# When VectorE reads the sums at the turn of the down projection's two passes, and which product a seven-product chunk begins with

## The chip, the cores and the metric

One core of a Trainium2 chip runs the whole program. The metric is the device time of one execution in microseconds (us), here the median of three runs. One further execution was taken by the hardware profiler; all rows below are from that one.

## What is computed

One decoder layer on 256 tokens of width 2048, in float32: a projection, two kinds of attention, an output projection, a layer norm, a gated FFN with a short convolution, and a second layer norm. The change lies in the FFN's second half alone:

```python
def conv_ffn(h, w_up, conv_w, conv_b, w_down):
    u = h @ w_up
    g, val = u[..., :FFN_DIM], u[..., FFN_DIM:]
    ...
    return (jax.nn.silu(gc) * val) @ w_down          # 256x5632 times 5632x2048

f = conv_ffn(h, w_up[l], conv_w[l], conv_b[l], w_down[l])
h = layer_norm(DEEPNORM_ALPHA * h + f, ln2_g[l], ln2_b[l])
```

## The kernel before

Each float32 factor is split into a rounded high part and the low rest (`hi`, `lo`), and a product is three matmuls: high by high, high by low, low by high. ScalarE (ACT) makes the high part, VectorE (DVE) subtracts to get the low one. All engines run instruction lists that the code writes out in order; an engine that waits for one instruction holds back all that stand behind it.

The down projection `act @ w_down` is done in two passes n = 0 and 1, one for each half of the 2048 output columns. A pass goes over 22 chunks p = 0 to 21 of 256 FFN features. "Chunk 0/21" below is chunk 21 of pass 0. A plain chunk (`mm_d`) is 24 matmuls, in 12 pairs that alternate between two PSUM banks: first the 12 of token row t = 0 (`bank[0]`, `bank[1]`; `CB[0]`), then the 12 of row t = 1 (`bank[2]`, `bank[3]`; `CB[1]`). The chunks that `SEVEN` lists (3, 6, 9, 12, 15, 18 in pass 0) are done by Strassen's scheme instead: `mm_seven` makes seven products of three matmuls, 21 in all. Its right-hand sides are seven blocks in the tile `slot`, 0 to 2 raw blocks of the weight chunk, 3 to 6 sums of blocks. The left-hand sides are blocks of activations or their sums (`sums`, with `sh` for the high and `sl` for the low parts). Products 1, 5, 6, 7 collect in banks 4, 5, 6, 7 (`MB`) and products 2, 3, 4 directly in the `CB` banks.

What a seven-product chunk s needs is made in the two chunks ahead of it. In `begin(s - 2)` ScalarE writes the negated high parts of raw blocks 0 to 2 into the low half of `slot` (L516), and a transfer issued by GpSimd's queue adds the raw blocks to them in place (L517): the low parts of blocks 0 to 2 come from this transfer. VectorE makes the sums (L519, L520, L492 to L495) there, and in `middle(s - 2)` their low parts (L529, L505), the next block sum (L536) and other splits. The last block follows in `begin(s - 1)`.

Weight chunks come into four `raw` buffers. SyncE's queue (SP) issues the load of chunk i + 6 in `begin(i)`; it waits there until the buffer of chunk i + 2 is free. For a seven-product chunk that is when L517's transfer and L536 have read it, and the loads behind it in SP's queue wait too. So loads go out in bursts of three, each begun when a transfer of L517 has landed. In chunk 1/9 the two vectors of the last layer norm (`load_gb`, L392, two transfers of 1024 KB) are issued as well.

At the turn of the passes the `CB` banks of pass 0 must be added into `z` (`z_add`, L871) before pass 1 writes them again. The code does it within chunk 0/21 and before chunk 1/0:

```python
            for k in range(2):
                mm_d(i, 0, [0, 1], k)
            if n == 0 and p == PT - 1:
                for c in range(2):
                    z_add(0, 0, c, CB[0][c])
            if i < last[0] - 1:
                middle(i)
            for k in range(2):
                mm_d(i, 1, [0, 1], k)
```

The two `z_add` of row 1 follow after that. `shared_out` adds the `MB` banks into `z` in the two chunks behind the last seven-product chunk of a pass, and `z_stats` takes statistics of `z` in the two chunks after the turn. The last four chunks of pass 1 run in another order (`mm_d` by column, `mm_d_end`) with high and low parts that are made in chunk 1/17 (tile `end`).

Of the kernel before, what the change touches and what calls it, by code (L numbers as in the profile page):

```python
# [41 lines left out]
PAIRED_END = 4  # L42
PT = FT // 2

SEVEN = (range(3, 19, 3), range(1, 14, 3))

ENDS = {(1, 1): ("cos_d", "sin_d"), (2, 0): ("mask", "cos_m"), (2, 1): ("sin_m", "lam4")}

# [2 lines left out]
def hymba_layer(ctx: ExitStack, tc: tile.TileContext, a: dict):  # L51
# [72 lines left out]
    def split(i, half, both=None):  # L124

        if i >= NS or (i, half) in parts:
            return
        t = loaded[i] if half == 0 else loaded.pop(i)
        if both is None:
            hi = splits.tile([P, 1024], F32R, name="hi")  # L130
            lo = splits.tile([P, 1024], F32R, name="lo")
        else:
            hi, lo = both[:, half], both[:, 2 + half]
        for x, y in pieces(i, half):
            if i < 4 and x % 512 == 0:
                split_x(4 * i + x // 512, 4 * i + (y + 511) // 512)
            s = slice(x - 1024 * half, y - 1024 * half)
            ACT.activation(hi[:, s], t[:, x:y], AF.Copy)  # L138
            DVE.tensor_tensor(lo[:, s], t[:, x:y], hi[:, s].bitcast(F32), ALU.subtract)  # L139
        parts[i, half] = (hi, lo)  # L140
# [101 lines left out]
    def at(step, fn, *args, rank=LATER):  # L242
        after.setdefault(step, []).append((rank, len(after.get(step, ())), fn, args))
# [144 lines left out]
    def load_gb(which, both):  # L388
        for j, n in enumerate(("g", "b")):
            t = both[:, j]  # L390
            src = a[f"ln{which}_{n}"]
            SP.dma_start(t, bass.AP(tensor=src.tensor, offset=src.offset, ap=[[0, P], [1, D]]))  # L392
            gb[n] = t
# [60 lines left out]
    def seven(i):  # L454
        return stream[i][0] == "d" and stream[i][1] in SEVEN[stream[i][2]]

# [16 lines left out]
    def split_act(i, k):  # L473

        if i >= NS or stream[i][0] != "d" or (i, k) in aparts:
            return
        src = act_of(2 * stream[i][1] + k)
        hi, lo = act_tiles(i, k)
        ACT.activation(hi, src, AF.Copy)
        DVE.tensor_tensor(lo, src, hi.bitcast(F32), ALU.subtract)  # L480
        aparts[i, k] = (hi, lo)
# [16 lines left out]
    def act_sums_split(i):  # L498
        f = sums[i]
        out = []  # L500
        for j in range(2):
            hi = keep.tile([P, 2, P], F32R, name="sh", tag=("mask", "cos_m")[j])
            lo = keep.tile([P, 2, P], F32R, name="sl", tag=("sin_m", "lam4")[j])
            ACT.activation(hi, f[j], AF.Copy)
            DVE.tensor_tensor(lo, f[j], hi.bitcast(F32), ALU.subtract)  # L505
            out += [(hi[:, k], lo[:, k]) for k in range(2)]

        sums[i] = out
# [17 lines left out]
    def blocks_lo(i, *js):  # L526
        slot, f = blocks[i]
        for j in js:
            DVE.tensor_tensor(slot[:, 1, 3 + j], f[j % 2 if j < 2 else 0], slot[:, 0, 3 + j].bitcast(F32),  # L529
                              ALU.subtract)  # L530

    def blocks_sum(i, j):

        t = loaded[i].rearrange("p (b c) -> p b c", c=512)
        f = blocks[i][1]
        DVE.tensor_tensor(f[0], t[:, 2 - j], f[0], ALU.subtract)  # L536
        if j == 1:
            loaded.pop(i)

    def blocks_hi(i, j):  # L540
        slot, f = blocks[i]
        ACT.activation(slot[:, 0, 5 + j], f[0], AF.Copy)
# [15 lines left out]
    def begin(i):  # L558

        urgent(i)  # L560
        j = i + 2
        split_act(j - 1, 1)
        split_act(j, 0)
        if j < NS and seven(j):
            blocks_raw(j)
            act_sums(j)
        elif j - 1 < NS and seven(j - 1):
            blocks_sum(j - 1, 1)
            split(j, 1)
            blocks_hi(j - 1, 1)  # L570
            blocks_lo(j - 1, 3)
        else:
            split(j, 1)
        load(i + 6)
        pending(i)

    def middle(i):

        urgent(i + 0.5)
        if i + 2 < NS and seven(i + 2):  # L580
            blocks_lo(i + 2, 0)
            blocks_sum(i + 2, 0)
            blocks_lo(i + 2, 1)
            act_sums_split(i + 2)
            blocks_hi(i + 2, 0)
            split(i + 3, 0)
            blocks_lo(i + 2, 2)
        elif i + 3 < NS and not seven(i + 3):
            split(i + 3, 0)
        pending(i + 0.5)  # L590

    def urgent(i):
        for _, _, fn, args in sorted((x for x in after.get(i, ()) if x[0] < LATER), key=lambda x: x[:2]):
            fn(*args)

    def pending(i):
        for x in after.pop(i, ()):
            if x[0] == LATER:
                x[2](*x[3])

    def done(i):
        for half in range(2):
            parts.pop((i, half))
# [68 lines left out]
    last = range(first_u - PAIRED, first_u)  # L672
# [169 lines left out]
    def mm_three(key, dst, lhs, rhs):  # L842
        for x, y in ((0, 0), (0, 1), (1, 0)):
            mm_count(key, dst, lhs[x], rhs[y])

    def mm_d(i, t, cs, k):

        n = stream[i][2]
        ts = slice(t * P, (t + 1) * P)
        ah, al = (x[:, ts] for x in aparts[i, k])  # L850
        w = [weights(i, (1536 * c if k == 0 else 512 + 512 * c), 512) for c in cs]
        for lhs, j in ((ah, 0), (ah, 1), (al, 0)):
            for c, wc in zip(cs, w):
                mm_count((n, t, c), CB[t][c], lhs, wc[j])

    def mm_seven(i):
        n = stream[i][2]
        slot, _ = blocks.pop(i)
        s3, s1, s2, s4 = sums.pop(i)
        (h0, l0), (h1, l1) = aparts[i, 0], aparts[i, 1]  # L860
        a11, a12, a22 = (h0[:, 0:P], l0[:, 0:P]), (h1[:, 0:P], l1[:, 0:P]), (h1[:, P:], l1[:, P:])
        for m, lhs, b in ((1, a11, 0), (2, a12, 1), (5, s1, 3), (7, s3, 4), (6, s2, 5), (3, s4, 2), (4, a22, 6)):
            t, c = {2: (0, 0), 3: (0, 1), 4: (1, 0)}.get(m, (None, None))
            key, dst = ((n, m), MB[m]) if t is None else ((n, t, c), CB[t][c])
            if m == 6:
                middle(i)
            mm_three(key, dst, lhs, (slot[:, 0, b], slot[:, 1, b]))

    def z_add(n, t, c, src, alpha=1.0):
        s = slice((2 * n + c) * 512, (2 * n + c + 1) * 512)  # L870
        DVE.scalar_tensor_tensor(z[:, t, s], z[:, t, s], alpha, src, op0=ALU.mult, op1=ALU.add)  # L871
# [23 lines left out]
    last = range(NS - PAIRED_END, NS)  # L895


    for n in range(2):
        np_ = PT if n == 0 else PT - PAIRED_END
        n7 = len(SEVEN[n])  # L900
        for m in MB:
# [18 lines left out]
    for i in range(first_d, NS - PAIRED_END):  # L920
        begin(i)
        _, p, n, _ = stream[i]
        if n == 1 and p == 9:
            load_gb(2, keep.tile([P, 2, D], F32, name="gb2", tag="ma"))
        if i == last[0] - 1:
            split_act(last[1], 1)
            for j, g in ((last[2], "t2"), (last[3], "mb")):
                end = keep.tile([P, 4, 1024], F32R, name="end", tag=g)
                for k in range(2):
                    split_act(j, k)  # L930
                    split(j, k, end)
        if seven(i):
            mm_seven(i)
            if p == SEVEN[n][-1]:
                at(i + 1, shared_out, n, 0)
                at(i + 2, shared_out, n, 1)
        else:
            for k in range(2):
                mm_d(i, 0, [0, 1], k)
            if n == 0 and p == PT - 1:  # L940
                for c in range(2):
                    z_add(0, 0, c, CB[0][c])
            if i < last[0] - 1:
                middle(i)
            for k in range(2):
                mm_d(i, 1, [0, 1], k)
            done(i)
            if n == 0 and p == PT - 1:
                for c in range(2):
                    z_add(0, 1, c, CB[1][c])  # L950
                for t in range(2):
                    for c in range(2):
                        at(i + 2 + t, z_stats, t, c, (512, 256)[t])
        for k in range(2):
            aparts.pop((i, k))
# [58 lines left out]
    for o in (1024, 1280):  # L1014
        s = slice(o, o + 256)
        b = bank[2][:, o - 1024:o - 768]
# [72 lines left out]
```

## Time and profile before

| what | value |
|---|---|
| median of 3 runs | 1144.22 us (1143.83 to 1145.06) |
| the profiled execution, its own time | 1144.3 us |
| its span, first to last instruction | 1142.5 us |
| TensorE (PE) busy | 1124.0 us, 98% |
| VectorE busy | 810.2 us, 71% |
| ScalarE busy | 614.6 us, 54% |
| granted TensorE clock, mean | 0.997 of full speed |

TensorE is busy in nearly all of the span, so what can be won without taking matmuls out is only the time in which it stands still; the places are few and can be looked at one by one.

### The profile page before, as it was taken

The page shows a single profiled execution, that of the slowest core. Times are in us where ns is not written, and L with a number is a line of the kernel's source. Part 1 is how long each engine was busy: PE and PEld are TensorE (multiplying, and loading weights), DVE is VectorE, ACT ScalarE, POOL GpSimd, SP SyncE. Part 2 cuts the span into 40 slices and gives each one's busy share as a digit, 9 for nine tenths or more (in the row PEclk, how much of TensorE's full clock was granted, in tenths as well). Part 3 has the DMA queues.
Part 4 walks back from the last instruction along what each step waited for, and adds up shares of the span by engine and source line. Part 5 has one row for each costly group of instructions (what it writes and reads, how often), then busy time and mean ns, then how long its engine had stood idle before and what let it go on. Part 6 is the DMA issues. An engine that isn't in the chain of part 4 may idle for free.

```text
span 1142.5 us, 15605 instructions
## 1 busy us (share of the span) xinstructions
PE 1124.0 (98%) x5971; PEld 961.2 (84%) x5971; DVE 810.2 (71%) x1373; ACT 614.6 (54%) x1007; POOL 30.2 (3%) x38
## 2 busy tenths in 40 slices
PE   9999999999999999999999999999999999999996
PEld 6888888888888898888888888888888888877785
DVE  6895886857745777777666566666656788898885
ACT  6565564444443485554545555454555667666751
POOL 0000000000000000000000000000000000000004
PEclk9999999999999999999999999999999999999998
DMA  9755454454455456555555555555555678877841
GB/s 319 292 221 193 151 182 167 165 184 175 157 184 184 185 200 231 194 186 185 184 190 193 202 189 184 185 186 191 192 202 178 208 210 254 277 197 227 279 173 74
DMA packets 47324, 226.56 MB, mean 198 GB/s; under 512 B 4625, under 2 KB 6545, under 8 KB 27665
## 3 DMA queue, kind: packets, MB, share of 16 engines
q1 hardware_dynamic: 45664, 216.92, 53.5%
q0 software_dynamic: 1584, 8.65, 3.8%
q8 instruction: 46, 0.75, 0.3%
q14 instruction: 30, 0.24, 0.1%
HBM read 214.80 MB, written 2.10 MB: 190 GB/s over the span
## 4 chain that ended last, share of the span: by engine, by line
PE 93%; DMA 3%; DVE 2%; ACT 1%; issue 0%; SPq 0%; POOL 0%; ACTq 0%
PE bank L206 92%; DMA slot<-raw 2%; DMA raw<-in_w_v 1%; PE bank L329 0%; DVE z L871 0%; DVE lo L139 0%; ACT slot L516 0%; ACT hi L138 0%; DVE z L976 0%; PE bank L705 0%; SPq L155 0%; PE bank L376 0%; SPq L121 0%; ACT hf L708 0%; DVE h L720 0%
## 5 line engine op out<-in xcount | busy, mean ns | idle before, releaser
L139 DVE TENSOR_TENSOR lo<-raw,hi 128x1024 fp32r<-128x1024 f32 (+1 forms) x372 | 440.8, 1200 | 216.5 <-ACT hi L138 216.2
L138 ACT ACTIVATE hi<-raw 128x1024 fp32r<-128x1024 f32 (+1 forms) x372 | 380.1, 1035 | 230.0 <-PE bank L206 198.3
L206 PE MATMUL bank<-h,hi 128*128 128x512 f32 x1376 | 477.2, 390 | 0.0
L206 PE MATMUL bank<-h,lo 128*128 128x256 f32 x1376 | 388.4, 282 | 0.0
L206 PEld LDWEIGHTS bank<-h,hi 128*128 128x128 f32 x1376 | 258.3, 188 | 53.4
L206 PEld LDWEIGHTS bank<-h,lo 128*128 128x128 f32 x1376 | 260.8, 190 | 0.0
L206 PE MATMUL bank<-x,hi 128*128 128x512 f32 x512 | 181.6, 396 | 0.0
L206 PE MATMUL bank<-x,lo 128*128 128x256 f32 x512 | 144.4, 282 | 0.0
L206 PEld LDWEIGHTS bank<-x,hi 128*128 128x128 f32 x512 | 96.2, 188 | 21.4 <-issue 1.3
L206 PEld LDWEIGHTS bank<-x,lo 128*128 128x128 f32 x512 | 97.0, 190 | 0.2
L206 PE MATMUL bank<-hi,x 128*128 128x512 f32 x256 | 85.3, 403 | 0.6 <-ACT hi L138 0.6
L206 PEld LDWEIGHTS bank<-hi,x 128*128 128x128 f32 x256 | 48.2, 188 | 13.3 <-ACT hi L138 2.1
L443 ACT ACTIVATE gc<-gs,vec 128x256 f32<-128x256 f32 x43 | 25.9, 602 | 58.6 <-DVE gs L220 58.6
L206 PE MATMUL bank<-lo,x 128*128 128x512 f32 x128 | 51.1, 399 | 0.8 <-DVE lo L139 0.8
L446 ACT ACTIVATE gc<-gc 128x256 f32<-128x256 f32 x44 | 18.4, 418 | 48.9 <-DVE gc L445 48.9
L206 PE MATMUL bank<-hi,ah 128*128 128x512 f32 (+1 forms) x126 | 40.6, 396 | 2.4 <-DVE z L871 2.3
L206 PE MATMUL bank<-hi,mh 128*128 128x512 f32 x128 | 42.2, 400 | 0.0
L206 PE MATMUL bank<-lo,mh 128*128 128x512 f32 x128 | 41.6, 396 | 0.0
L206 PE MATMUL bank<-hi,ml 128*128 128x512 f32 x128 | 41.6, 396 | 0.0
L444 DVE SCALAR_TENSOR_TENSOR gc<-gs,vec,gc 128x255 f32<-128x255 f32 x43 | 20.8, 484 | 28.8 <-ACT gc L443 28.8
L206 PE MATMUL bank<-lo,ah 128*128 128x512 f32 (+1 forms) x126 | 39.7, 390 | 0.0
L206 PE MATMUL bank<-hi,al 128*128 128x512 f32 (+1 forms) x126 | 39.7, 390 | 0.0
(176 smaller groups left out, 1284.9 us busy)
## 6 DMA issues: line engine op xcount, KB each, us to landing
raw<-in_w_u SPq DMA_DIRECT2D x88, 1024.0 KB, 4.8
raw<-in_w_d SPq DMA_DIRECT2D x88, 512.0 KB, 5.9
raw<-in_w_qk SPq DMA_DIRECT2D x32, 1024.0 KB, 4.8
raw<-in_w_o SPq DMA_DIRECT2D x16, 1024.0 KB, 4.8
raw<-in_w_v SPq DMA_DIRECT2D x12, 1024.0 KB, 4.8
slot<-raw POOLq DMA_DIRECT2D x11, 768.0 KB, 7.3
raw<-in_w_v SPq DMA_DIRECT2D x8, 256.0 KB, 5.6
raw<-in_w_v SPq DMA_DIRECT2D x4, 512.0 KB, 7.7
```

What stands on the lines that cost most here:

```text
L138: ACT.activation(hi[:, s], t[:, x:y], AF.Copy)
L139: DVE.tensor_tensor(lo[:, s], t[:, x:y], hi[:, s].bitcast(F32), ALU.subtract)
L206: PE.matmul(out, lhsT, rhs, start=start, stop=stop)
L443: ACT.activation(gc, g, AF.Identity, bias=vec[:, C_CB + f:C_CB + f + 1], scale=w[2])
L444: DVE.scalar_tensor_tensor(gc[:, 1:], g[:, 0:S - 1], w[1], gc[:, 1:], op0=ALU.mult, op1=ALU.add)
L446: ACT.activation(gc, gc, AF.Silu)
```

## The change

Three edits. In pass 1 the seven-product chunks move by one, from 1, 4, 7, 10, 13 to 2, 5, 8, 11, 14. In every seven-product chunk, of both passes, products 5 and 7 come first, ahead of 1 and 2. And in chunk 0/21 `middle` is called after the `z_add` of row 1 and not between the two rows.

```diff
-SEVEN = (range(3, 19, 3), range(1, 14, 3))
+SEVEN = (range(3, 19, 3), range(2, 15, 3))
...
-        for m, lhs, b in ((1, a11, 0), (2, a12, 1), (5, s1, 3), (7, s3, 4), (6, s2, 5), (3, s4, 2), (4, a22, 6)):
+        for m, lhs, b in ((5, s1, 3), (7, s3, 4), (1, a11, 0), (2, a12, 1), (6, s2, 5), (3, s4, 2), (4, a22, 6)):
...
             if n == 0 and p == PT - 1:
                 for c in range(2):
                     z_add(0, 0, c, CB[0][c])
-            if i < last[0] - 1:
+            elif i < last[0] - 1:
                 middle(i)
             for k in range(2):
                 mm_d(i, 1, [0, 1], k)
...
             if n == 0 and p == PT - 1:
                 for c in range(2):
                     z_add(0, 1, c, CB[1][c])
+                middle(i)
                 for t in range(2):
```

VectorE's list at the turn, before: `bank_72` to `bank_75` are the `CB` banks 0 to 3 (row 0, then row 1), `slot`, `tf`, `sl` belong to the seven-product chunk 1/1, `lo<-raw` is the low part of a plain chunk's weights.

```order
L871 SCALAR_TENSOR_TENSOR z<-z,bank_72 128x512
L871 SCALAR_TENSOR_TENSOR z<-z,bank_73 128x512
L529 TENSOR_TENSOR slot<-tf,slot 128x512
L536 TENSOR_TENSOR tf<-raw,tf 128x512
L529 TENSOR_TENSOR slot<-tf,slot 128x512
L505 TENSOR_TENSOR sl<-sf,sh 128x256 x2
L139 TENSOR_TENSOR lo<-raw,hi 128x1024
L529 TENSOR_TENSOR slot<-tf,slot 128x512
L871 SCALAR_TENSOR_TENSOR z<-z,bank_74 128x512
L871 SCALAR_TENSOR_TENSOR z<-z,bank_75 128x512
```

The same place of the changed kernel, from the end of `shared_out` (the first row adds its last part) on; the two `lo` are those of chunk 1/1, which is a plain chunk now:

```order
L871 SCALAR_TENSOR_TENSOR z<-z,act_6820 128x512 x2
L139 TENSOR_TENSOR lo<-raw,hi 128x1024
L480 TENSOR_TENSOR bl<-act_3772,bh 128x256
L480 TENSOR_TENSOR al<-act_3772,ah 128x256
L139 TENSOR_TENSOR lo<-raw,hi 128x1024
L871 SCALAR_TENSOR_TENSOR z<-z,bank_72 128x512
L871 SCALAR_TENSOR_TENSOR z<-z,bank_73 128x512
L871 SCALAR_TENSOR_TENSOR z<-z,bank_74 128x512
L871 SCALAR_TENSOR_TENSOR z<-z,bank_75 128x512
L480 TENSOR_TENSOR bl<-act_3772,bh 128x256
L480 TENSOR_TENSOR al<-act_3772,ah 128x256
L519 TENSOR_TENSOR tf<-raw 128x512
```

Nothing stands between the rows of `z` any more, the two low parts of weights stand ahead of them, and the sums that now belong to chunk 1/2 stand behind.

TensorE's list in a seven-product chunk, the difference (`bank_77` and `bank_79` are banks 5 and 7, products 5 and 7; `bank_76` is product 1, `bank_72` product 2):

```order
+L206 MATMUL bank_77<-slot,sh 128x512 x2
+L206 MATMUL bank_77<-slot,sl 128x512
+L206 MATMUL bank_79<-slot,sh 128x512 x2
+L206 MATMUL bank_79<-slot,sl 128x512
 L206 MATMUL bank_76<-slot,ah 128x512 x2
 L206 MATMUL bank_76<-slot,al 128x512
 L206 MATMUL bank_72<-slot,bh 128x512 x2
 L206 MATMUL bank_72<-slot,bl 128x512
-L206 MATMUL bank_77<-slot,sh 128x512 x2
-L206 MATMUL bank_77<-slot,sl 128x512
-L206 MATMUL bank_79<-slot,sh 128x512 x2
-L206 MATMUL bank_79<-slot,sl 128x512
```

Six matmuls on sums of blocks moved ahead of the first product that reads a low part of a raw block.

## Rows read from the trace of the kernel before

**Rows 1.** The page's first line.
```profile
span 1142.5 us, 15605 instructions
```

**Rows 2.** Waits of PE: who for whom, us in total, times, longest.
```profile
PE bank L206 <- DVE z L871: 2.3, 1, 2.3
PE bank L206 <- DMA slot<-raw: 1.7, 2, 1.3
```

**Rows 3.** Timeline of PE at the turn: start us, us, instruction, count.
```profile
1004.59 0.64 PE L206 MATMUL bank<-hi,ah 128*128 128x512 f32 x2
...
1007.36 0.64 PE L206 MATMUL bank<-hi,ah 128*128 128x512 f32 x2
...
1009.66 0.61 PE L206 MATMUL bank<-hi,bl 128*128 128x512 f32 x2
1012.62 1.09 PE L206 MATMUL bank<-hi,ah 128*128 128x512 f32 x2 [2.35 <-DVE z L871]
1013.55 0.62 PE L206 MATMUL bank<-lo,ah 128*128 128x512 f32 x2
```

**Rows 4.** Timeline of PE where chunks 1/7 and 1/13 begin.
```profile
1047.77 0.40 PE L206 MATMUL bank<-slot,ah 128*128 128x512 f32 x1
...
1048.94 0.39 PE L206 MATMUL bank<-slot,al 128*128 128x512 f32 x1
...
1080.39 0.40 PE L206 MATMUL bank<-slot,ah 128*128 128x512 f32 x1
...
1082.41 0.39 PE L206 MATMUL bank<-slot,al 128*128 128x512 f32 x1
```

**Rows 5.** Stretches: us, busy of PE, PEld, DVE, ACT, POOL, PEclk, DMA share, GB/s.
```profile
1007.36:1015.85 8.49, 6.04 (x26) 4.43 (x24) 8.08 (x14) 4.74 (x8) 0.00 (x0) 1.00 0.25 46
```

**Rows 6.** Timeline of DVE at the turn.
```profile
1001.75 1.29 DVE L871 SCALAR_TENSOR_TENSOR z<-z,act 128x512 f32<-128x512 f32 x2
1002.96 0.42 DVE L480 TENSOR_TENSOR bl<-act,bh 128x256 fp32r<-128x256 f32 x1
1003.29 0.42 DVE L480 TENSOR_TENSOR al<-act,ah 128x256 fp32r<-128x256 f32 x1
...
1010.14 1.23 DVE L139 TENSOR_TENSOR lo<-raw,hi 128x1024 fp32r<-128x1024 f32 x1 [0.37 <-ACT hi L138]
1011.28 0.68 DVE L529 TENSOR_TENSOR slot<-tf,slot 128x512 fp32r<-128x512 f32 x1
1011.89 1.28 DVE L871 SCALAR_TENSOR_TENSOR z<-z,bank 128x512 f32<-128x512 f32 x2
```

**Rows 7.** The chain that ended last: start us, us, what.
```profile
1039.12 9.44 DMA slot<-raw
...
1071.75 10.28 DMA slot<-raw
```

**Rows 8.** Timeline of ACT, the split that follows chunk 0/19.
```profile
996.26 1.06 ACT L138 ACTIVATE hi<-raw 128x1024 fp32r<-128x1024 f32 x1 [3.33 <-PE bank L206]
```

**Rows 9.** Line L517, from issue to landing of its 11 transfers.
```profile
DMA to landing us min/median/max: 5.7/7.3/10.3
```

**Rows 10.** SP's issues: a weight chunk is L114 and L115.
```profile
1036.33 0.38 SPq L114 DMA_DIRECT2D raw<-in_w_d  x1
...
1063.40 0.38 SPq L114 DMA_DIRECT2D raw<-in_w_d  x1
...
1065.34 0.74 SPq L392 DMA_DIRECT2D gb<-in_ln_g  x1
...
1067.85 0.38 SPq L114 DMA_DIRECT2D raw<-in_w_d  x1
```

**Rows 11.** Timeline of DVE: sums' low parts for 1/4; the first `end` part.
```profile
1027.39 0.76 DVE L505 TENSOR_TENSOR sl<-sf,sh 128x256 fp32r<-128x256 f32 x2
...
1108.12 1.22 DVE L139 TENSOR_TENSOR end<-raw,end 128x1024 fp32r<-128x1024 f32 x1
```

**Rows 12.** Timeline of PE, the first matmul that reads `end`.
```profile
1111.77 1.56 PE L206 MATMUL bank<-end,eh 128*128 128x512 f32 x6
```

## The prediction

> **What bounds the kernel now.** I read the page's busy shares first: the span is 1142.5 us [rows 1] and TensorE is busy in 98% of it. The change takes no matmul out, so it can win only where TensorE stands still. The view of waits therefore came next, for PE alone. Of its waits two lines lie in the part of the program that changes: 2.3 us, once, for a `z_add`, and 1.7 us in two pieces for the transfer into `slot` [rows 2]. The timeline of PE then gives the true price of each, because a wait also costs a slow restart. A pair of matmuls takes 0.46 us: from 1007.36 to 1009.66 there are five pairs in 2.30 us [rows 3].
>
> - The turn: from the last pair of row 0 in chunk 1/0 (1009.66) to the second pair of row 1 (1013.55) it is 3.89 us, where two pairs take 0.92 [rows 3]. Lost: 2.97 us.
> - Chunk 1/7: from the first matmul (1047.77) to the third (1048.94) it is 1.17 us instead of 0.46 [rows 4]. Lost: 0.71 us.
> - Chunk 1/13: 1080.39 to 1082.41, 2.02 us [rows 4]. Lost: 1.56 us.
>
> Together 5.24 us. The granted clock stayed at 1.00, the level of 2.4 GHz, in the stretch that holds the longest of these stops [rows 5], so no gain or loss by the clock is to be added.
>
> **The turn, part by part.** Row 1 of chunk 1/0 may start when VectorE has read banks 2 and 3. These were complete when chunk 0/21 ended, at about 1007.4, but the reads ran only from 1011.89 on, since the block sums, a weight split and their waits for ScalarE stood ahead of them; TensorE restarted at 1012.62, when the first of the two was through [rows 3, 6]. The change puts `middle` behind the reads and, by moving the seven-product chunk from 1/1 to 1/2, also takes the sums of `begin(0/21)` out of the way. What stands there now is a plain chunk's preparation: two `lo`, one ahead and one behind a `bl` and `al`. I work out when VectorE comes to each read.
>
> The first `hi` of chunk 1/1 needs the split buffer of chunk 0/20. One chunk earlier ScalarE began the like at 996.26, as soon as PE released it [rows 8]; a plain chunk is 12 pairs, 5.54 us, so it begins at 1001.80 and ends at 1002.86. VectorE finishes `shared_out` at 1003.04 [rows 6], so ScalarE is not late. From start to start a `lo` takes 1.14 us (1010.14 to 1011.28), `bl` and `al` 0.33 each (1002.96 to 1003.29), the two adds of a row 1.28 [rows 6]. Hence 1003.04 + 1.14 + 0.67 + 1.14 = 1005.99 for the first read of row 0, and 1007.27 for the end of the second. TensorE wants bank 0 at 1007.36 and bank 1 a matmul (0.23 us) later [rows 3]: 0.3 us to spare at bank 1, 0.7 at bank 0. This is tight, and it is a rival below. Row 1 is complete at about 1007.5, its reads end at 1008.8, and TensorE wants bank 2 at 1010.12 (1007.36 plus six pairs): 1.3 us to spare. I take the whole 2.97 us as gained; the bounds are nothing (the wait returns in full at row 0) and 2.97.
>
> What goes late instead: the sums for 1/2 begin behind these reads, at 1008.8, which is 1.4 us into chunk 1/0; even counted from that chunk's start they are no more than 1.4 us late. For 1/4 the low parts of the sums were ready at 1027.39 + 0.76 = 1028.15 [rows 11], and that chunk began 15.96 us (two plain chunks and 21 products) before 1/7, at 1031.81 [rows 4]. That leaves 3.7 us, which covers it. Cost taken: 0. If the cover were gone, each us would be a us of TensorE.
>
> **Products 5 and 7 first.** They read only sums, not the blocks whose low parts the transfer writes. Before, the second matmul needed the transfer: in 1/13 it was due at 1080.62, 8.87 us after the issue at 1071.75 [rows 4, 7]. Now six matmuls, three pairs or 1.38 us, come ahead, so the transfer may take 10.25 us. It took 9.44 ahead of 1/7 and 10.28 ahead of 1/13 [rows 7], and 7.3 in the median of 11 [rows 9]. With the same transfers the 0.71 us vanishes and of the 1.56 us some 0.03 stays.
>
> They need not be the same transfers, since the chunks move. Why was the last one slow? The loads begun at 1063.40 included the two vectors of 1024 KB from 1065.34 on and a further weight chunk at 1067.85 [rows 10]: five transfers' worth ahead of it instead of three. After the change the burst ahead of 1/14 holds the same five, the vectors merely one place further forward, and starts when the transfer of 1/11 has landed. Ahead of 1/7 the third load came late, at 1036.33, 2.8 us before the issue [rows 7, 10]; for 1/5 the first two of the statistics of `z` now stand ahead of the split that frees its buffer, so it will be late again, by about as much. I expect 9.4 to 10.3 us at both, a wait of 0 to 0.1. Below, a gain is bounded by zero wait. Above, I let either transfer take 1.5 us longer than the slowest seen, which would leave a wait as long as that of 1/13.
>
> Here a rule of the Trainium skill can be weighed. The two slow transfers end about 6 us after the last load queued ahead must have drained, as if they ran behind the loads [rows 7, 10]. "DMA: Bandwidth & Descriptors", section "Queues, rings and completion order", says that each DMA engine takes turns between the queues packet by packet, and its section "Anatomy of one DMA — SWDGE (gpsimd) path" fits about 2.0 us plus the bytes over 436 GB/s. With half the bandwidth that would be an estimate of 5.6 us for 768 KB, and no wait at all in 1/7 and 1/13. By that page nothing of the two waits would stay after the change either, and the sum would be lower by the 0.1 us that I leave; the trace disagrees on the time (9.44 and 10.28).
>
> **Tail.** `shared_out` of pass 1 moves one chunk closer to the end. Its last part, four operations of VectorE at about 0.64 (1.28 for two [rows 6]), 2.6 us, is queued in chunk 1/16 now and not in 1/15, a chunk ahead of the `end` splits. Those begin at 1108.12, and TensorE reads the first at 1111.77 [rows 11, 12]; the `lo` itself takes 1.23 [rows 6], so VectorE may be 2.4 us later there than now, even before what the chunk between takes up. Cost 0; without that chunk it would be 0.2. In pass 0 only the order of products changes, and no wait stood there: 0.
>
> **Sum.** 1144.3 (the profiled execution's own time) - 2.97 - 0.71 - 1.56 + 0.1 = 1139.16, say 1139.1. That execution is 0.1 above the median of the runs shown, 1144.22, so against the median it is the same to what can be told. The span should be near 1137.4.
>
> **Rivals.**
> - *The wait moves to row 0 of chunk 1/0.* For it speaks that only 0.3 us is spare, and that four instructions, one of them started by PE's release of a buffer, must run without a gap. Against it, that ScalarE has 0.2 us in hand on VectorE. A delay of 1 us gives about 1139.9; if all of 2.97 returns, 1142.1. Chance 0.10.
> - *The transfer is later where the chunks now lie*, at 1/5 behind the statistics or at 1/14 behind the vectors. For it speaks the burst, against it that the 1/14 burst starts no later relative to its chunk than that of 1/13. One wait of 1.5 us gives 1140.6, two give 1142.1. Chance 0.14.
> - *The change doesn't do what it says*: some other reader holds bank 2 or the restart. PE's wait names the add, and it ended with the first of the two reads [rows 2, 3, 6]. It would give 1142.1, the two transfers' gain alone. Chance 0.02.
> - *Slower: sums late in every chunk.* All 11 seven-product chunks now need the low parts of the sums at their start and not 1.38 us later. They were ready 3.7 us ahead for 1/4 [rows 4, 11], a chunk that had the statistics in its way. If VectorE came so late that each chunk waited x us, the price is 11x; from x = 0.48 it eats the whole gain, and at 1 us the time is 1150.1. The point is a delay of 4.2 us. Chance 0.03.
>
> **How the numbers follow.** My forecast, all three stops gone but for 0.1 or little more, has 0.71; 1139.1, within 1138.5 and 1139.9. A measurement of this kernel can tell about 0.2%, 2.3 us, so faster is under 1141.9. The first two rivals fall under it except at their far ends: faster 0.71 + 0.08 + 0.12 = 0.91; same 0.02 + 0.02 + 0.02 = 0.06; slower 0.03. The range from 1138.4 to 1140.9 takes in the forecast, a wait of 1.5 us at one transfer and half the first rival; it leaves out the two dear ends, the third rival and the slow side, less than 0.2.
>
> **What would show it.** Right: no wait of PE for L871; VectorE's four adds of the `CB` banks in one run from about 1006 to 1008.8; the first matmul of each seven-product chunk at the pace of the pair before it; at most 0.1 us of wait for `slot`, and then at the eighth matmul of 1/5 or 1/14. Wrong: PE waiting at the first pair of 1/0, transfers above 10.25 us, or a PE wait for L505 or L529 where a seven-product chunk starts.

## The result, and the profile after

| | before | after |
|---|---|---|
| median | 1144.64 us (4 runs, 1143.83 to 1145.45) | 1139.38 us (4 runs, 1139.14 to 1140.41) |
| span of the profiled execution | 1142.5 us | 1137.5 us |

The ratio is 0.9949, 95% interval 0.9936 to 0.9962: 5.3 us less. The forecast was 1139.1 us and a span of 1137.4.

The page of the changed kernel, its first lines (busy us, share, instructions): TensorE is busy for as long as before, in a span 5 us shorter.

```profile
span 1137.5 us, 15607 instructions
...
PE 1124.0 (99%) x5971; PEld 962.2 (85%) x5971; DVE 810.0 (71%) x1373; ACT 614.7 (54%) x1007; POOL 30.1 (3%) x38
```

All waits of PE in the changed kernel. Neither of the lines of [rows 2] is left; these three lie ahead of the down projection. Of the weight loads' waits (PEld) one is still for `slot`.

```profile
PE bank L206 <- DVE idle L546: 1.2, 1, 1.2
PE bank L206 <- DVE h L720: 0.7, 1, 0.7
PE bank L206 <- ACT hi L138: 0.6, 1, 0.6
```

```profile
PEld bank L206 <- DMA slot<-raw: 0.6, 1, 0.6
```

The turn, timeline of DVE in the changed kernel, which answers to [rows 6]:

```profile
1002.89 1.22 DVE L139 TENSOR_TENSOR lo<-raw,hi 128x1024 fp32r<-128x1024 f32 x1
1004.03 0.42 DVE L480 TENSOR_TENSOR bl<-act,bh 128x256 fp32r<-128x256 f32 x1
1004.36 0.42 DVE L480 TENSOR_TENSOR al<-act,ah 128x256 fp32r<-128x256 f32 x1
1004.70 1.22 DVE L139 TENSOR_TENSOR lo<-raw,hi 128x1024 fp32r<-128x1024 f32 x1
1005.84 1.28 DVE L871 SCALAR_TENSOR_TENSOR z<-z,bank 128x512 f32<-128x512 f32 x2
1007.26 1.28 DVE L871 SCALAR_TENSOR_TENSOR z<-z,bank 128x512 f32<-128x512 f32 x2 [0.15 <-PE bank L206]
1008.47 0.42 DVE L480 TENSOR_TENSOR bl<-act,bh 128x256 fp32r<-128x256 f32 x1
```

VectorE now waits 0.15 us for TensorE to end row 1 of chunk 0/21, where before TensorE waited for VectorE. The timeline of PE over the same place answers to [rows 3]: row 1 of chunk 1/0 follows row 0 at the pace of the pairs.

```profile
1007.30 0.64 PE L206 MATMUL bank<-hi,ah 128*128 128x512 f32 x2
...
1009.60 0.62 PE L206 MATMUL bank<-hi,bl 128*128 128x512 f32 x2
1010.06 0.64 PE L206 MATMUL bank<-hi,ah 128*128 128x512 f32 x2
1010.54 0.62 PE L206 MATMUL bank<-lo,ah 128*128 128x512 f32 x2
```

What is left of [rows 4] is one short stop in the last seven-product chunk, 1/14 (timeline of PE), and the transfer behind it (chain that ended last: start, us):

```profile
1083.54 1.01 PE L206 MATMUL bank<-slot,ah 128*128 128x512 f32 x2
1084.39 0.39 PE L206 MATMUL bank<-slot,al 128*128 128x512 f32 x1
```

```profile
1073.51 10.50 DMA slot<-raw
```

The pair took 0.85 us instead of 0.46, so 0.39 us are lost there. The gain worked out from the stops is then 2.97 + 0.71 + 1.56 - 0.39 = 4.85 us; the spans differ by 5.0. A fourth stop of the kernel before lies in pass 0 and is too small for the view of waits: at chunk 0/6, behind a transfer of 8.8 us, the first pair took 0.58 us (937.87 to 938.45) instead of 0.46. In the changed kernel it is gone, which adds 0.12 us: 4.97 in all.

### The profile page after: what moved, and what is told of

It is laid out like the page before. It is cut to its first block, busy times and chain, and to the rows that moved or that the text cites. A ratio compares the mean times of both kernels' runs of the same rounds, so it can differ in the third digit from the quotient of the medians.

```text
span 1137.5 us, 15607 instructions
## 1 busy us (share of the span) xinstructions
PE 1124.0 (99%) x5971; PEld 962.2 (85%) x5971; DVE 810.0 (71%) x1373; ACT 614.7 (54%) x1007; POOL 30.1 (3%) x38
## 4 chain that ended last, share of the span: by engine, by line
PE 97%; DMA 1%; DVE 1%; ACT 0%; issue 0%; POOL 0%; SPq 0%; ACTq 0%
PE bank L206 96%; DMA slot<-raw 1%; PE bank L329 0%; DMA raw<-in_w_v 0%; DVE z L977 0%; PE bank L705 0%; PE bank L376 0%; ACT hf L708 0%; ACT slot L516 0%; DVE h L720 0%; DVE st L400 0%; DVE z L397 0%; POOL rstd L408 0%; DVE z L1019 0%; DVE bank L1018 0%
```

## The experiments

**The chunks' move alone.** VectorE's list is that of the changed kernel, since `middle` has nothing to do in chunk 0/21 once 1/1 is a plain chunk and 1/2 a seven-product one; the products keep their old order.

```diff
-SEVEN = (range(3, 19, 3), range(1, 14, 3))
+SEVEN = (range(3, 19, 3), range(2, 15, 3))
```

> Only the seven-product chunks of pass 1 move to 2, 5, 8, 11, 14; products 1 and 2 stay first, and the code still calls middle between the rows of z. My theory: the move alone frees the turn, since with it VectorE's list is that of the changed kernel, the four adds of the banks in one run; PE's wait for L871 is gone (2.97 us gained). The waits for the transfer into slot stay, because without products 5 and 7 ahead a transfer may take only 8.87 us: with transfers as in the changed kernel (9.0, 8.5, 7.3, 10.5 us in pass 1) about 0.1 at 1/5 and 1.7 at 1/14, so 2.97 + 2.27 - 1.8 = 3.4 us gained, time about 1141.2. Rival, that the turn needs the third edit as well: wait for L871 of over 1 us, time 1143 or more. Rival, that the transfers were only slow by chance and are hidden anyway: 1139.3, as the changed kernel.

Measured: 1141.23 us, ratio 0.9966 (0.9953 to 0.9979). The wait for L871 is gone, and `slot` is waited for in two places, here the greater, at 1/14 (timeline of PE):

```profile
1082.47 0.40 PE L206 MATMUL bank<-slot,ah 128*128 128x512 f32 x1
1084.75 0.50 PE L206 MATMUL bank<-slot,ah 128*128 128x512 f32 x1 [1.88 <-DMA slot<-raw]
```

The transfers in pass 1 took 6.6, 9.3, 8.8, 8.4 and 10.9 us; those clearly above 8.87 us are the ones that were waited for. The two stops cost 0.55 and 2.16 us, more than the 1.8 expected; that the time came out as expected is in part luck. Beside the move the third edit does nothing.

**The order of products alone.**

```diff
-        for m, lhs, b in ((1, a11, 0), (2, a12, 1), (5, s1, 3), (7, s3, 4), ...
+        for m, lhs, b in ((5, s1, 3), (7, s3, 4), (1, a11, 0), (2, a12, 1), ...
```

> Only the order of the products changes: 5 and 7 first, in both passes; the chunks and the turn are those of before. My theory: the two waits for slot go (2.2 us gained), PE's wait of 2.3 us for L871 stays, time about 1142.2. Rival, that products 5 and 7 find their sums late: waits of PE for L505 or L529, time 1144 or more. Rival, that transfers get slower with this order (in the changed kernel those of pass 0 took 9.3 to 10.1 us against 6.8 to 8.8 before): waits for slot at some chunks of pass 0 again, time 1143.

Measured: 1143.74 us, ratio 0.9989 (0.9978 to 0.9999), a span of 1142.0. Less than expected, and none of the three theories had the cause. The waits for `slot` are down to 0.2 us and nothing waits for sums, as expected. But behind the stop at the turn the matmuls ran at less than full clock (timeline of PE, and the stretch with its PEclk, the third number from the end):

```profile
1012.37 1.10 PE L206 MATMUL bank<-hi,ah 128*128 128x512 f32 x2 [2.35 <-DVE z L871]
1013.31 0.94 PE L206 MATMUL bank<-lo,ah 128*128 128x512 f32 x2
1014.05 1.05 PE L206 MATMUL bank<-hi,al 128*128 128x512 f32 x2
1014.90 1.05 PE L206 MATMUL bank<-hi,bh 128*128 128x512 f32 x2
1015.75 1.05 PE L206 MATMUL bank<-lo,bh 128*128 128x512 f32 x2
1016.61 0.75 PE L206 MATMUL bank<-hi,bl 128*128 128x512 f32 x2
```

```profile
1012.37:1016.60 4.23, 4.13 (x10) 3.00 (x11) 4.23 (x7) 1.58 (x2) 0.00 (x0) 0.63 0.32 63
```

A pair starts every 0.85 us there, where [rows 3] have 0.46. The granted clock is 0.63 on the mean, so most of the stretch is at the lower of the two levels, 1.2 GHz. From 1009.41, the start of the pair ahead of the stop, to 1017.19, the first product of 1/1, it is 7.78 us for seven pairs, 4.56 us lost and not 2.97: the fall of the clock cost another 1.6 us. The profiled execution of before had the same wait and kept its clock [rows 5].

**The third edit alone.**

```diff
-            if i < last[0] - 1:
+            elif i < last[0] - 1:
                 middle(i)
...
                     z_add(0, 1, c, CB[1][c])
+                middle(i)
```

> Only the third edit: middle is called after the adds of row 1; chunks 1, 4, 7, 10, 13 and the old order of products stay. My theory: this alone frees the turn too, since the block sums stand behind the adds and chunk 1/1 begins with raw blocks whose transfer was issued long ahead; the last block sum is ready at about 1016.6, half a us before product 4 reads it. Time about 1144.6 - 2.97 = 1141.6, no wait for L871, at most 0.5 us of wait for L529 in 1/1. Rival, that the move of the chunks is what frees the turn: the sums for 1/1 come too late, PE waits 2 us or more for L505, L529 or L542's block, time 1143.5 or more.

Measured: 1142.83 us, ratio 0.998 (0.9972 to 0.9989), span 1141.0. My theory held for the turn: no wait for L871, none for L529 in 1/1. It missed the next chunk (timeline of PE at 1/4):

```profile
1028.57 0.40 PE L206 MATMUL bank<-slot,ah 128*128 128x512 f32 x1
1030.96 0.50 PE L206 MATMUL bank<-slot,ah 128*128 128x512 f32 x1 [1.99 <-DMA slot<-raw]
1031.29 0.39 PE L206 MATMUL bank<-slot,al 128*128 128x512 f32 x1
```

Here 2.72 us are spent on 0.46 of work. The transfer ahead of 1/4 was issued at 1019.92, only 0.8 us behind the third load of the burst, and took 11.0 us (issues of POOL and of SP):

```profile
1019.92 0.87 POOL L517 DMA_DIRECT2D slot<-raw  x1 [15.37 <-ACT slot L516]
```

```profile
1014.48 0.38 SPq L114 DMA_DIRECT2D raw<-in_w_d  x1
...
1019.12 0.38 SPq L114 DMA_DIRECT2D raw<-in_w_d  x1
```

The first of these loads waits for VectorE's last block sum of 1/1 (the transfer ahead of it had landed at 1009.5), the third for a split of weights. Both went out when they did in the kernel before (1014.50 and 1019.15), but TensorE, no longer stopped, came earlier, and with it the transfer's issue (1023.16 before). Three quarters of the stop moved from the turn to 1/4; at 1/13 1.72 us are lost, at 1/7 nothing.

**The vectors later, in the kernel before.**

```diff
-        if n == 1 and p == 9:
+        if n == 1 and p == 15:
             load_gb(2, ...)
```

> The kernel of before with the last layer norm's two vectors loaded in chunk 1/15, not in 1/9. My theory: they are what made the transfer ahead of 1/13 take 10.28 us; without them it takes about 7.5 us, as ahead of 1/10, and PE's wait at 1/13 (1.56 us lost) goes; that at 1/7 (0.71) stays. Time about 1143.1. Rival, that the transfer is slow for another reason (its own read and write, its place in the pass): still about 10 us and the wait stays, time 1144.6.

Measured: 1142.71 us, ratio 0.9982 (0.9971 to 0.9994), span 1140.8. The transfer ahead of 1/13, L517 of a window there, and the first matmuls of that chunk:

```profile
slot<-raw POOLq DMA_DIRECT2D x1, 768.0 KB, 7.7
```

```profile
1080.29 0.63 PE L206 MATMUL bank<-slot,ah 128*128 128x512 f32 x2
1080.75 0.39 PE L206 MATMUL bank<-slot,al 128*128 128x512 f32 x1
```

10.28 became 7.7 us and the stop is gone; that at 1/7 stays, with 0.58 us lost. The vectors ahead in the queues were the cause: in the ten profiled executions here that have them in the last burst its transfer took 10.3 to 11.6 us, in the two without them 7.7 and 8.3.

**The vectors later, in the changed kernel** (the same edit).

> The changed kernel with the two vectors of the last layer norm loaded in chunk 1/15 and not in 1/9. My theory: the transfer ahead of 1/14, 10.50 us in the changed kernel, falls to 7.5 to 9 us, and with it the last stop of PE in the down projection (0.39 us lost at 1083.54). Span about 1137.1, time about 1139.0, which no timing can tell from the changed kernel; the rows can. Rival, that the transfer is slow by its place ahead of the last seven-product chunk: still above 10.25 us and the stop stays.

Measured: 1137.74 us, ratio 0.9936 (0.9924 to 0.9948); the transfer ahead of 1/14 took 8.3 us (the queues' view), and no wait for `slot` is left on PE or PEld.

```profile
slot<-raw POOLq DMA_DIRECT2D x1, 768.0 KB, 8.3
```

The changed kernel beside it, next, gave 1139.35; the intervals overlap, so the times alone do not tell the two apart, but the row with the stop is gone. Its median is the lowest of the versions here.

**The changed kernel again.**

> The changed kernel once more, on the chip of the runs beside it. If a stop of PE at the turn costs more than its wait, because the clock falls behind it in some executions (0.63 of full speed over 4.23 us in the run with the order alone, 1.9 us lost), then this kernel, without that stop, shows a mean clock of 0.997 in nearly every run and a spread of about 1 us, where the kernel before shows 0.994 to 0.997 and a spread of 3 us or more. Rival, that the clock falls by chance anywhere: 0.995 in as many of its runs as before. Time 1139.3 either way or, with falls, up to 1141.

Measured: 1139.35 us (1137.84 to 1139.85, 5 runs), ratio 0.9944 (0.9932 to 0.9956). The 1.9 us named above come to 1.6 when they are counted from the stop to the start of chunk 1/1, as was done for the run with the order alone. 1/14 waits again, 0.5 us behind a transfer of 10.9. Each run has a mean clock. In the 19 runs of the changed kernel, of this one, of the one with the vectors later and of the one that follows it is 0.996 or 0.997 without exception. In 58 runs of the kernel before that stand beside the experiments it is 0.994 or 0.995 in 44, with a median of 1145.2 us, and 0.996 or 0.997 in 14, with a median of 1143.7. The spread of before was 2.4 to 6.1 us in sets of 12 to 31 runs, here 2.0 in 5; with so few runs that proves little.

A mean clock does not say where the clock was low. Every trace here ends in 5 to 9 us at the lower level, behind the last matmul, and that alone takes the mean to 0.997 or 0.996. The run with the order alone, with its fall of 1.6 us at the turn, shows 0.996 too. So 0.996 does not rule out a fall, and 0.995 does not place one at the turn.

**Two more operations of VectorE ahead of the reads of row 0.** Nothing reads what they write.

```diff
             if n == 0 and p == PT - 1:
+                for k in range(2):
+                    pad = work.tile([P, 512], F32, name="pad", tag="m1")
+                    h = weights(i + 1, 1024 * k, 512)[0].bitcast(F32)
+                    DVE.tensor_tensor(pad, h, h, ALU.add)
                 for c in range(2):
                     z_add(0, 0, c, CB[0][c])
```

> The changed kernel with two more operations of VectorE (each 512 wide, about 0.6 us, on data that nothing reads) ahead of the reads of row 0 at the turn. My theory, that only 0.4 us is spare there: the reads end 1.2 us later, at 1008.3 instead of 1007.05, PE wants bank 1 at 1007.53, so it waits for L871 and loses 0.8 to 1.3 us: span 1138.3 to 1138.8. Rival, that there is more room (PE's queue or a later need of bank 1): no wait for L871, span 1137.5.

Measured: 1140.28 us (4 runs), span 1138.6. Timeline of DVE and of PE:

```profile
1005.68 1.29 DVE L944 TENSOR_TENSOR pad<-hi 128x512 f32<-128x512 f32 x2
1006.89 2.48 DVE L871 SCALAR_TENSOR_TENSOR z<-z,bank 128x512 f32<-128x512 f32 x4
```

```profile
1006.68 0.61 PE L206 MATMUL bank<-hi,bl 128*128 128x512 f32 x2
1007.71 1.08 PE L206 MATMUL bank<-hi,ah 128*128 128x512 f32 x2 [0.42 <-ACT ah L479]
1008.63 0.63 PE L206 MATMUL bank<-lo,ah 128*128 128x512 f32 x2
```

From 1006.68 to 1008.63 it is 1.95 us for two pairs, 1.03 lost. The releaser that the row names, an `ah`, ended at 1003.3 and cannot be it; the first add started at 1006.89 and takes about 0.68, and PE goes on at 1007.71, just behind its end. The two operations took 1.21 us, and the second read, which ends at about 1008.17, comes 0.80 us after chunk 1/0 would have wanted bank 1 (1007.14, a pair behind 1006.68, plus a matmul). So the room at row 0 was 0.4 us, as small as was worked out.

**The second and third edits without the move** (the chunks stay at 1, 4, 7, 10, 13).

> Second and third edits without the move of the chunks (they stay at 1, 4, 7, 10, 13). With the third edit alone the wait for L871 was gone, but the transfer ahead of 1/4 took 11.0 us and PE waited 2.0 us there and 1.4 at 1/13. My theory: 1.38 us more room takes the first to about 0.8 us and the second to about 0.1; the move of the chunks is then worth that 1 us, not the turn. Time about 1140.3, span 1138.5. Rival, that chunk 1/1 now needs its sums too early (PE waits for L505 or L529 over 0.5 us): 1141 or more.

Measured: 1141.87 us, ratio 0.9967 (0.9956 to 0.9979), span 1138.5. PE waits at 1/4 and at 1/13 (timeline at 1/4, then 1/13):

```profile
1029.69 0.50 PE L206 MATMUL bank<-slot,ah 128*128 128x512 f32 x1 [0.75 <-DMA slot<-raw]
...
1079.44 0.50 PE L206 MATMUL bank<-slot,ah 128*128 128x512 f32 x1 [1.25 <-DMA slot<-raw]
```

No wait for sums. The first is what was expected, the second larger: the transfers of pass 1 took 5.7, 11.1, 10.5, 9.6 and 11.6 us, a late one making the next burst late. At 1/4 and 1/13 1.02 and 1.50 us are lost, 2.1 more than in the changed kernel. The median is 1.6 us above what I expected and 2.5 above the changed kernel beside it, so the move of the chunks is worth 2 to 2.5 us: not by the turn, but by keeping the transfers behind it early.

**Six more operations ahead of the reads of row 0** (the edit above with `range(6)`, and `k % 2` for the block that is read), which puts the stop back.

> The changed kernel with six more operations of VectorE (3.6 us, on data that nothing reads) ahead of the reads of row 0 at the turn, which puts a stop of PE there again. The reads of row 0 end 3.2 us after PE wants bank 1, so PE loses about 3.2 us at row 0 and a little at row 1: span 1140.7 to 1141.2 where the clock holds. My theory, that the stop makes the clock fall behind it in many executions: mean clock 0.995 in half of the runs or more, and those about 1.7 us longer than the rest. Rival, that the fall in the kernel before has another cause: 0.996 to 0.997 in all runs, as in the changed kernel.

Measured: 1143.43 us (11 runs), ratio 0.9986 (0.9977 to 0.9995). PE's wait for L871 is 2.8 us, in the profiled execution with the clock at 1.00 around it (span 1140.4; timeline of PE, and the stretch):

```profile
1009.10 1.07 PE L206 MATMUL bank<-hi,ah 128*128 128x512 f32 x2 [2.82 <-DVE z L871]
```

```profile
1005.00:1012.00 7.00, 4.05 (x17) 2.88 (x16) 7.00 (x14) 2.10 (x3) 0.87 (x1) 1.00 0.86 220
```

Of the 11 runs 5 have a mean clock of 0.994 or 0.995, with a median of 1144.4 us; the other six have 0.996 or 0.997 and 1142.4. The stop brings the lower mean clock back, in about half of the runs, which are about 2 us longer. That the clock is low right behind the stop in those five is not shown: the one trace is of a run without a fall.

**The statistics later, in the kernel before.**

```diff
-                        at(i + 2 + t, z_stats, t, c, (512, 256)[t])
+                        at(i + 6 + t, z_stats, t, c, (512, 256)[t])
```

> The kernel before with the statistics of z taken four chunks later. My theory: they made the third load ahead of 1/7 late and with it the transfer into slot (9.44 us). Without them the load goes out about 1.1 us earlier and the transfer takes 8.3 us or less, so no wait at 1/7; 1/13 keeps its 1.6 us. Rival, that the transfer of 1/7 is slow for another reason: 9.3 us and a wait of 0.4 to 0.7 us again.

Measured, one execution: 1147.34 us, span 1145.5. The transfer ahead of 1/7 took 6.7 us and its wait is gone, as expected. The statistics now stand ahead of the third load for 1/10, and the delay goes on from there: 9.5 us ahead of 1/10, 11.2 ahead of 1/13. The wait at 1/13 is greater than before (timeline of PE), and the clock fell twice, at the turn and there (stretches, PEclk third from the end):

```profile
1083.56 0.79 PE L206 MATMUL bank<-slot,ah 128*128 128x512 f32 x1 [2.22 <-DMA slot<-raw]
```

```profile
1011.65:1016.29 4.64, 4.64 (x12) 3.42 (x13) 4.64 (x7) 1.78 (x3) 0.00 (x0) 0.63 0.28 75
1079.00:1089.00 10.00, 7.78 (x28) 5.93 (x27) 6.54 (x9) 4.19 (x6) 0.00 (x0) 0.83 0.94 294
```

The third load ahead of 1/7 went out 3.9 us ahead of the transfer's issue (1035.65 and 1039.57), where it was 2.8 in the kernel before. The fall of the clock at the turn is not what made that room: with the order alone the clock fell there too, and it was 2.8 (1037.66 and 1040.43). So the statistics were the cause at 1/7, as far as one execution shows; taking them away there only passed the delay on to where the vectors' load makes it dear.

## Why the prediction was right

- *Three stops and nothing else.* Shown, but for 0.12 us at chunk 0/6: pass 0 was taken to have no wait. The page has the same busy time of PE, and the waits for L871 and for `slot` are gone but for 0.39 us. The sum took 5.14 us away and the stops give 4.97, because that term and the 0.3 us too little at 1/14 partly cancel. That the medians agree with the forecast to 0.3 us is in part luck, as single runs of the changed kernel lie 1.3 us apart; the rows carry the argument.
- *The turn, 2.97 us.* Right in size and mechanism. VectorE's reads were worked out for 1005.99 and 1007.27 and for an end at 1008.8; they ran from 1005.84, ended at 1007.12 for row 0 and at about 1008.5 for row 1. The spare time at bank 1 was put at 0.3 us; with two more operations it comes out at 0.4. The prediction gave the credit to `middle` and the chunks' move together. The runs with one edit show that either does it alone, and that beside the move `middle` has nothing left to do.
- *Products 5 and 7 first, 1.38 us more room.* Right: the transfer may take 10.25 us, those of 9.0 and below went by unseen, that of 10.50 was waited for. With the order alone the waits for `slot` fell from 1.7 to 0.2 us.
- *The transfers after the move, 9.4 to 10.3 us and a wait of 0 to 0.1.* Mis-sized: 9.0 at 1/5, but 10.50 at 1/14, and 0.39 lost. In the experiments that left the vectors in that burst the transfer behind it took 10.4 to 11.6. The cause named, the vectors in the burst, was shown by loading them later: 10.28 to 7.7 in the kernel before, 10.50 to 8.3 in the changed one. The prediction read that the slow transfers end about 6 us after the last load ahead must have drained. That does not hold: the last load ahead of 1/13 went out at 1068.27 and landed 15.7 us later, after the transfer, which ended at 1082.03; ahead of 1/7 the distance is 4.2 us. What the trace of before shows at 1/13 is a late start. The queues' view (packets, MB, share of the DMA engines; q1 carries SP's loads, q0 the transfer) for the 3.5 us behind the issue at 1071.75, and then to the transfer's end:

```profile
q1 hardware_dynamic: 199, 1.50, 102.7%
```

```profile
q0 software_dynamic: 144, 0.79, 56.7%
q1 hardware_dynamic: 406, 1.12, 44.6%
```

For 3.5 us loads alone moved, then the transfer went, beside loads. Ahead of 1/1, with the load of one chunk under way, it started 1.0 us after its issue and landed after 5.7. The page of the Trainium skill that was weighed, "DMA: Bandwidth & Descriptors", section "Queues, rings and completion order", would have a transfer take its turns beside the loads; by the estimate that the prediction works out with it, 5.6 us, none of these stops would be there. The 3.5 us without a turn do not agree with it, unless the transfer's packets were not yet in their queue, which no row shows. The transfers follow what is queued ahead of them: 5.7 to 6.7 us in all runs with one chunk's load (the first of pass 1), 10.3 to 11.6 behind the burst with the vectors.
- *Tail and sums at no cost.* Right: no PE wait for L505, L529 or a part of `end`.
- *No clock term.* Right for the two profiled executions, both at 0.997, and so for the sum made against them. It is not the whole: in 44 of 58 other runs of before the mean clock is lower, and against those the change gains 1.5 us more.

## What to carry to other kernels

Where one engine is busy for 98% of the time, list its stops in the timeline with the slow restart in them, and ask of each what stands ahead of the releasing instruction in its own queue; the sum of three such stops gave the result to 0.3 us. A stop that is taken away lets the next transfer be issued earlier against loads that did not move: work out who comes too early then, as the run with the third edit alone shows. Reordering the consumer, so that work with other inputs comes first, was enough to hide most of a late transfer; moving the load that makes it late hid the rest.

## What the runs showed that I had not expected

- A stop of TensorE of 2.35 us was followed by a granted clock of 0.63 over 4.2 to 4.6 us in two profiled executions, at a cost of 1.6 us in one of them, and by 1.00 in others with the same wait. A mean clock of 0.994 or 0.995 stands in 44 of 58 runs of the kernel before, in 5 of 11 where a stop of 2.8 us was put back, and in none of 19 with the whole change (four of them with the stop of 1.0 us). The stop at the turn is not all of it. It is there with the order alone and with the vectors later in the kernel before, which lack both or one of the stops at `slot`, and there 5 of 12 and 3 of 10 runs are low; with the third edit alone, where the longest wait is 1.99 us, at 1/4, it is 2 of 12. The moved chunks alone (longest wait 1.88 us) have 0 of 8, the second and third edits (1.25) 0 of 5. In the run with the statistics later the clock fell behind the wait of 2.22 us at 1/13 too. What decides in a single execution stays open.
- In pass 0 the six transfers into `slot` of the changed kernel took 6.0, 7.0, 9.4, 10.1, 9.3 and 9.7 us, and when it was run again 6.0, 6.7, 9.4, 10.1, 9.4 and 10.1; with the same instructions there, the kernel with the vectors later had 6.1, 6.3, 7.3, 6.3, 6.8 and 7.5. They cost nothing, as they are under 10.25 us; at a limit of 8.87 us they would have cost. The traces show where it begins. In seven of the twelve, these two and that of before among them, the second load of the burst ahead of the third transfer went out 1.9 to 2.5 us behind the first, and that transfer took 8.6 to 9.4 us; in the other five it was 1.1 us behind, and 6.5 to 7.4. In the changed kernel the next bursts, begun when a transfer has landed, were late in turn; the kernel before recovered (7.3). Why the load was late in some was not looked for.
- The part ahead of the down projection, the same in all kernels here, varied: the first transfer of L517 was issued at 897.2 us in the changed kernel's profile and at 895.8 when it was run again. Spans of single executions tell no difference below some 1.5 us; their rows do.
